# A decoder layer on one core: FFN up and gate token-major, 512 columns at a time, turned back by VectorE and small DMAs

## The chip, the cores and the metric

The kernel runs on one core of one Trainium2 chip. The metric is the device time of one execution in microseconds (us). Three executions of the kernel before took 447.74, 448.15 and 448.26 us, median 448.15. The trace comes from one more execution, with the profiler on, which took 447.88 us; the part of it that the instructions span is 446.0 us.

Engines are named as the profile names them: PE is TensorE's matmul stream, PEld its weight loads, DVE is VectorE, ACT is ScalarE, POOL is GpSimd, SP is SyncE. SPq is SP's queue, which issues nearly all DMAs.

## The reference

One layer of a decoder trunk, float32, 256 tokens (S), model width 1024 (D), FFN width 2816. The second half, which the change touches, is:

```python
    x = x + jnp.einsum('bsd,de->bse', merged, w_out[l])
    h = rmsnorm(x, norm2_g[l])
    up = causal_dwconv(jnp.einsum('bsd,df->bsf', h, w_up[l]), ffn_conv_w[l], ffn_conv_b[l])
    act = jax.nn.gelu(up) * jnp.einsum('bsd,df->bsf', h, w_gate[l])
    x = x + jnp.einsum('bsf,fd->bsd', act, w_down[l])
```

`causal_dwconv` is a convolution over three successive tokens, with its own three weights and bias per channel. The first half, called the mixers here, is a projection to 7168 columns, a gated linear recurrence (rx, rg, ri), an attention with 8 heads (q, k, v), two branch gates (ga, gb), two branch projections (pr, pa) and the output projection (wo).

## The kernel before, in words

**Precision.** Every float32 operand is split into a rounded part `hi` and the rest `lo`. Each product is three matmuls (`mm3`, lines 240 to 243): stationary hi with moving hi, hi with lo, lo with hi. A profile line L241, L242 or L243 is one of these three.

**The weight stream.** All weights come as 1 MB chunks, 128 partitions by 2048 columns, numbered in the order of use (`stream`, lines 173 to 198). For a chunk SP issues a load into a `raw` buffer (`load_next`, lines 203 to 213; 3 buffers), ScalarE casts it to `hi` (line 223; 4 buffers) and VectorE subtracts to get `lo` (line 224; 3 buffers). `advance(i)` (line 226) emits the loads and splits up to chunk `i`; loads are emitted up to 3 chunks ahead of the splits. A `raw` buffer becomes free when its chunk is split, a `hi` or `lo` buffer when TensorE has used the chunk.

**Two forms of matmul.** In the channel-major form (`fm_mm`, line 245) the weights are stationary (128x128) and the activations move, 256 tokens at a time: each matmul has 256 columns, and the result has channels on the partitions and tokens along the free axis. In the token-major form (`tm_mm`) the activations are stationary, 128 tokens at a time, and the weights move, 512 columns at a time; the result has tokens on the partitions. With `split=True` the 512 columns are two runs of 256 from one chunk, which holds half the contraction of two 256-column blocks (`two`, line 179). The mixers use the token-major form for q, k, v, ga, gb, pr and pa, the channel-major one for rx, rg and ri. The down projection and wo use `rows_mm` (line 664), 512 columns wide as well.

**The FFN** (lines 770 to 793). There are NF = 11 blocks of 256 channels. Block j does `up` (48 matmuls of 256 columns), `gate` (48), and then the down projection of block j-1 (24 matmuls of 512 columns), which adds into four PSUM banks `acc` that stay open to the end. `up_post` (line 740) multiplies `up` by the norm's factor per token (`rbf`, line 743), does the convolution along the free axis (one ScalarE pass, line 747, and two VectorE passes, line 751, per 128 channels) and the GELU (line 753). `gate_post` (line 756) multiplies by `gate` and splits the product into the operand of the down projection. All of this has channels on the partitions, where conv weights and biases are one number per partition. Block 0 is done in two halves of the contraction, since the last transposes of the normed activations (`norm2_t`, line 680) come between them; `norm2_bcast` (line 726) makes `rbf` with a small matmul.

**Order.** The mixers run as units of four quarters (`run_unit`). After each quarter, `run` emits the work that the table `AFTER` lists for it: `s24` is `advance(24)`, `P0` is an attention step, and so on. The table was written by an offline planner. Before the change it covers the mixers and wo; the FFN is a plain loop in which the splits run two chunks ahead (`AHEAD_S`). When the program is built, a list scheduler settles each engine's queue: emission order is the priority, and an instruction that is not ready by the builder's own reckoning lets later ones pass. Once built, each queue runs in its order.

**Buffers.** `half` is a pool of 22 buffers of 128x1024. PSUM has 4 banks in pool `psA` (long accumulations) and 4 in `psB` (`bank`).

Of the kernel before, what the change touches and what calls it, by code (L numbers as in the profile page):

```python
# [15 lines left out]
P = 128  # L16
S = 256
# [16 lines left out]
UNITS = ("rx0 rx1 rx2 rx3 rg0 rg1 rg2 rg3 k0 k1 k2 k3 ri0 q0 q1 ri1 q2 q3 v0 v1 v2 v3 ga0 ga1 ga2 ga3 gb0 "  # L34
         "gb1 gb2 gb3 pr0 pr1 pr2 pr3 pa0 pa1 pa2 pa3")
AFTER = {
    "rx0.0": "stats",
    "rg0.0": "s4",
    "rg0.2": "bcast evac1 s5",
    "rg0.3": "s6",  # L40
    "rg1.1": "evac0 evac2",
    "rg1.2": "evac3",
    "rg1.3": "conv0 decay",
    "rg2.0": "s7",
    "rg2.2": "conv1",
    "rg2.3": "s8 split0",
    "k0.1": "s9",
    "k0.2": "s10",
    "k0.3": "conv2 s11",
    "k1.0": "conv3 split1",  # L50
    "k1.3": "s12",
    "k2.3": "s13",
    "ri0.1": "s14",
    "ri0.2": "krs",
    "q0.0": "gelu1",
    "q0.1": "la0 lb0",
    "q0.2": "s15",
    "q1.0": "lc0",
    "q1.2": "s16",
    "q1.3": "s17",  # L60
    "ri1.0": "s18",
    "ri1.3": "ld0 la1",
    "q2.2": "lb1",
    "q3.1": "Tq0 ks0",
    "q3.2": "s19 ks1",
    "q3.3": "s20 qrs gelu0",
    "v0.2": "Tk0",
    "v0.3": "s21",
    "v2.0": "S0",
    "v2.1": "s22",  # L70
    "v2.2": "s23",
    "v3.1": "Tk1",
    "v3.3": "S1 S2",
    "ga0.2": "s24 P0",
    "ga0.3": "s25 lc1 s26 S3",
    "ga1.1": "P1 O0",
    "ga1.3": "Tq1",
    "ga2.1": "P2",
    "ga2.3": "P3",
    "ga3.0": "s27",  # L80
    "ga3.1": "O1",
    "ga3.2": "S6",
    "ga3.3": "S7 O3",
    "gb0.0": "O2 ya0 S4",
    "gb0.1": "S5",
    "gb0.2": "s28",
    "gb1.0": "P6",
    "gb1.2": "ld1 ya1 s29",
    "gb1.3": "P4",
    "gb2.0": "sa1",  # L90
    "gb2.1": "P7 O4",
    "gb2.2": "s30",
    "gb2.3": "ys1",
    "gb3.1": "ys0",
    "gb3.2": "P5",
    "gb3.3": "O6",
    "pr0.0": "s31 sb0",
    "pr0.1": "s32 O5",
    "pr0.2": "O7",
    "pr0.3": "s33",  # L100
    "pr1.2": "sa0",
    "pr2.2": "s34",
    "pr3.2": "s35",
    "pa0.0": "s36",
    "pa1.0": "s37",
    "pa1.3": "s38",
    "pa2.1": "s39",
    "pa2.3": "sb1",
    "pa3.2": "m0",
    "pa3.3": "m1 s40",  # L110
    "wo.3": "m3 s41",
    "wo.5": "m2",
    "wo.11": "n00",
    "wo.12": "s42 n10",
    "wo.15": "n01 s43",
}


# [1 line left out]
def trunk_layer(ctx: ExitStack, tc: tile.TileContext, xT, x, vec, win_fm, win_tm, wri, wpr, wpa,  # L120
# [10 lines left out]
    def half(name, dt=F32):  # L131
        return halfp.tile([P, 1024], dt, tag="half", name=name)
# [7 lines left out]
    def kt(t):  # L140
        return t.rearrange("p (k t) -> p k t", t=S)
# [49 lines left out]
    c_up, c_gt, c_dn = [], [], []  # L191
    for j in range(NF):
        c_up.append(add(wup[j]))
        c_gt.append(add(wgate[j]))
        if j >= 1:
            c_dn.append(add(wdown[j - 1]))
    c_dn.append(add(wdown[NF - 1]))
    last = len(stream) - 1

    raw, hi, lo = {}, {}, {}  # L200
# [56 lines left out]
    def fm_ps(name):  # L257
        return kt(bank(name))
# [421 lines left out]
    def norm2_t(t, hf):  # L680
        ps = bank(f"h2T{t}{hf}").rearrange("p (k t) -> p k t", k=4)
        ts = slice(t * P, (t + 1) * P)
        for k4 in range(4):
            k = 4 * hf + k4
            nc.tensor.transpose(ps[:, k4, :], xs[:, t, k * P:(k + 1) * P], ident)
        for k4 in range(4):
            k = 4 * hf + k4
            g = pv[:, V_G2 + k:V_G2 + k + 1]
            nc.scalar.activation(h2h[k][:, ts], ps[:, k4, :], AF.Copy, scale=g)
            nc.vector.scalar_tensor_tensor(h2l[k][:, ts], ps[:, k4, :], g, f(h2h[k][:, ts]),  # L690
                                           op0=OP.mult, op1=OP.subtract)
        nc.scalar.activation(small(f"sq2{t}{hf}", 512), xs[:, t, halves[hf]], AF.Square,
                             accum_out=ss2[:, hf, t:t + 1])
# [32 lines left out]
    def norm2_bcast():  # L726
        nc.vector.tensor_add(ss2[:, 0, :], ss2[:, 0, :], ss2[:, 1, :])
        rsqrt(ss2[:, 0, :], rs2, 1.0 / D, 2)
        for t in range(2):
            nc.vector.tensor_scalar(dg[:, t, :], ident, rs2[:, t:t + 1], None, op0=OP.mult)  # L730
        ps = bank("rbfp")
# [5 lines left out]
    acc = {(t, hf): psA.tile([P, 512], F32, tag="A", name=f"acc{t}{hf}") for t in range(2) for hf in range(2)}  # L737
    act = {}

    def up_post(j, ps):  # L740
        uc = half(f"fuc{j}")
        u, c = kt(uc[:, :512]), kt(uc[:, 512:])
        nc.vector.tensor_mul(u, ps, rbf2)  # L743
        for i in range(2):
            m = 2 * j + i
            w = lambda k: pv[:, V_FW + 3 * m + k:V_FW + 3 * m + k + 1]
            nc.scalar.activation(c[:, i, :], u[:, i, :], AF.Identity, scale=w(2),  # L747
                                 bias=pv[:, V_FB + m:V_FB + m + 1])
            for k in (1, 0):
                d = 2 - k  # L750
                nc.vector.scalar_tensor_tensor(c[:, i, d:], u[:, i, :S - d], w(k), c[:, i, d:],  # L751
                                               op0=OP.mult, op1=OP.add)
        nc.scalar.activation(c, c, AF.Gelu_apprx_tanh)
        return c

    def gate_post(j, c, ps):
        nc.vector.tensor_mul(c, c, ps)
# [12 lines left out]
    for j in range(NF):  # L770
        pu, pg = fm_ps(f"up{j}"), fm_ps(f"gt{j}")
        if j == 0:

            advance(c_up[0] + AHEAD_S)
            for half_k in range(2):
                ks = range(4 * half_k, 4 * half_k + 4)
                for ps, i in ((pu, c_up[0]), (pg, c_gt[0])):
                    fm_mm(ps, i, h2h, h2l, ks, True)
                    if not half_k and ps is pu:
                        norm2_t(1, 1)  # L780
            norm2_bcast()
            gate_post(0, up_post(0, pu), pg)
        else:
            advance(c_up[j] + AHEAD_S)
            fm_mm(pu, c_up[j], h2h, h2l)
            c = up_post(j, pu)
            advance(c_gt[j] + AHEAD_S)
            fm_mm(pg, c_gt[j], h2h, h2l)
            gate_post(j, c, pg)
            advance(c_dn[j - 1] + AHEAD_S)  # L790
            for t in range(2):
                for hf in range(2):
                    down(j - 1, t, hf)
    add_out(1, halves[1], acc[1, 1])
    advance(c_dn[NF - 1])
    for t in range(2):
# [75 lines left out]
```

## Time and profile before

| | us |
|---|---|
| median of 3 runs | 448.15 |
| profiled execution | 447.88 |
| its span | 446.0 |
| PE busy | 440.8 (99%) |
| DVE busy | 313.8 (70%) |
| ACT busy | 261.5 (59%) |
| mean DMA rate | 182 GB/s |

In a row of the timeline the columns are start, duration, engine, line, operation, output and inputs, tile sizes and count. In a row of the groups (lines) the columns are line, engine, operation, output and inputs, shapes, count, then busy us and mean ns of one, then the idle time of the engine just before these instructions and what ended it. Matmuls overlap each other in the array, so the distance between two starts, not the duration of one, is what a matmul costs.

### The profile page before, as it was taken

The numbers are of one execution on the slowest core, as the hardware profiler recorded it, in microseconds if no ns is written. First come the engines' busy times: TensorE is split into PE (matmuls) and PEld (weight loads), VectorE is DVE, ScalarE is ACT, GpSimd is POOL, SyncE is SP. The second block draws the span as 40 slices with busy tenths as digits, with TensorE's granted clock in tenths as the row PEclk, the third lists the DMA queues.
The fourth block names the chain that finished last, engine by engine and source line by source line (L and its number), as shares of the span: only waits on it lengthen the run. The fifth ranks groups of instructions, "written<-read, shape, count | busy, mean of one in ns | idle before, by whom it ended". The sixth has DMA issues, their size and how long they took to land.

```text
span 446.0 us, 6672 instructions
## 1 busy us (share of the span) xinstructions
PE 440.8 (99%) x2736; PEld 397.3 (89%) x2736; DVE 313.8 (70%) x462; ACT 261.5 (59%) x319; POOL 1.6 (0%) x9
## 2 busy tenths in 40 slices
PE   8999999999999999999999999999999999999996
PEld 8999988888888888888888899999999999999995
DVE  4688996979999775755677888575576575575553
ACT  4687757999996799733141656454354454454420
POOL 1000000000000000000000000000000000000000
PEclk9999999999999999999999999999999999999999
DMA  7995554645575455445545356545645645545202
GB/s 226 373 340 215 216 191 147 205 173 158 181 228 167 127 181 188 155 132 196 191 175 179 114 191 248 195 143 190 220 140 190 216 157 185 202 173 190 94 1 94
DMA packets 17629, 81.24 MB, mean 182 GB/s; under 512 B 1728, under 2 KB 4160, under 8 KB 10944
## 3 DMA queue, kind: packets, MB, share of 16 engines
q1 hardware_dynamic: 16880, 80.22, 51.9%
q10 hardware_dynamic: 720, 0.61, 0.5%
q8 instruction: 21, 0.34, 0.3%
q14 instruction: 8, 0.07, 0.0%
HBM read 79.78 MB, written 1.05 MB: 181 GB/s over the span
## 4 chain that ended last, share of the span: by engine, by line
PE 91%; ACT 5%; DMA 2%; issue 0%; DVE 0%; SPq 0%; ACTq 0%
PE gt L241 5%; PE gt L243 5%; PE gt L242 5%; PE up L243 5%; PE up L242 5%; PE up L241 5%; PE acc L241 4%; PE acc L242 4%; PE acc L243 4%; DMA raw<-in_win_fm 2%; PE rg L241 2%; PE rg L242 2%; PE rg L243 2%; PE ga L241 2%; PE gb L241 2%; PE pr L241 2%
## 5 line engine op out<-in xcount | busy, mean ns | idle before, releaser
L223 ACT CAST hi<-raw 128x2048 fp32r<-128x2048 f32 (+3 forms) x88 | 138.1, 1579 | 100.9 <-PE up L242 32.5
L224 DVE TENSOR_TENSOR lo<-raw,hi 128x2048 fp32r<-128x2048 f32 (+3 forms) x92 | 171.1, 1870 | 32.3 <-PE acc L242 14.0
L241 PE MATMUL up<-h2h,hi 128*128 128x256 f32 x176 | 49.9, 284 | 0.0
L241 PE MATMUL gt<-h2h,hi 128*128 128x256 f32 x176 | 49.9, 283 | 0.0
L243 PE MATMUL up<-h2h,lo 128*128 128x256 f32 x176 | 49.8, 283 | 0.0
L243 PE MATMUL gt<-h2h,lo 128*128 128x256 f32 x176 | 49.8, 283 | 0.0
L242 PE MATMUL gt<-h2l,hi 128*128 128x256 f32 x176 | 49.8, 283 | 0.0
L242 PE MATMUL up<-h2l,hi 128*128 128x256 f32 x176 | 49.8, 283 | 0.0
L241 PEld LDWEIGHTS up<-h2h,hi 128*128 128x128 f32 x176 | 33.7, 192 | 0.4
L242 PEld LDWEIGHTS up<-h2l,hi 128*128 128x128 f32 x176 | 33.7, 192 | 0.3
L242 PEld LDWEIGHTS gt<-h2l,hi 128*128 128x128 f32 x176 | 33.8, 192 | 0.0
L241 PEld LDWEIGHTS gt<-h2h,hi 128*128 128x128 f32 x176 | 33.8, 192 | 0.0
L243 PEld LDWEIGHTS gt<-h2h,lo 128*128 128x128 f32 x176 | 33.8, 192 | 0.0
L243 PEld LDWEIGHTS up<-h2h,lo 128*128 128x128 f32 x176 | 33.7, 192 | 0.0
L241 PE MATMUL acc<-hi,fa 128*128 128x512 f32 x86 | 33.6, 391 | 0.0
L242 PE MATMUL acc<-lo,fa 128*128 128x512 f32 x86 | 33.6, 390 | 0.0
L243 PE MATMUL acc<-hi,fa 128*128 128x512 f32 x86 | 33.5, 389 | 0.0
L743 DVE TENSOR_TENSOR fuc<-up,rbf 128x512 f32<-128x512 f32 x11 | 7.6, 691 | 33.2 <-PE up L243 33.2
L243 PEld LDWEIGHTS acc<-hi,fa 128*128 128x128 f32 x86 | 16.1, 188 | 3.5
L751 DVE SCALAR_TENSOR_TENSOR fuc<-fuc,pv 128x255 f32<-128x255 f32 (+1 forms) x44 | 18.6, 479 | 0.8 <-ACT fuc L747 0.7
L241 PEld LDWEIGHTS acc<-hi,fa 128*128 128x128 f32 x86 | 16.2, 188 | 3.1
L242 PEld LDWEIGHTS acc<-lo,fa 128*128 128x128 f32 x86 | 16.2, 188 | 2.9
(220 smaller groups left out, 1011.1 us busy)
## 6 DMA issues: line engine op xcount, KB each, us to landing
raw<-in_win_tm SPq DMA_DIRECT2D x12, 1024.0 KB, 4.8
raw<-in_win_fm SPq DMA_DIRECT2D x11, 1024.0 KB, 5.7
raw<-in_wup SPq DMA_DIRECT2D x11, 1024.0 KB, 4.8
raw<-in_wgate SPq DMA_DIRECT2D x11, 1024.0 KB, 4.8
raw<-in_wdown SPq DMA_DIRECT2D x11, 1024.0 KB, 4.8
raw<-in_wpr SPq DMA_DIRECT2D x4, 1024.0 KB, 4.9
raw<-in_wpa SPq DMA_DIRECT2D x4, 1024.0 KB, 4.9
raw<-in_wout SPq DMA_DIRECT2D x4, 1024.0 KB, 4.8
```

The lines of the kernel that those rows point to most:

```text
L223: (nc.vector.tensor_copy if on_dve else nc.scalar.copy)(hi[i][:, s], raw[i][:, s])
L224: nc.vector.tensor_sub(lo[i][:, s], raw[i][:, s], f(hi[i][:, s]))
L241: nc.tensor.matmul(o, ah, bh, start=start, stop=False, skip_group_check=skip)
L242: nc.tensor.matmul(o, ah, bl, start=False, stop=False, skip_group_check=skip)
L243: nc.tensor.matmul(o, al, bh, start=False, stop=stop, skip_group_check=skip)
L743: nc.vector.tensor_mul(u, ps, rbf2)
L751: nc.vector.scalar_tensor_tensor(c[:, i, d:], u[:, i, :S - d], w(k), c[:, i, d:], op0=OP.mult, op1=OP.add)
```

## The change

1. **Up and gate in pairs of blocks.** Ten of the eleven blocks are taken as five pairs of 512 channels. Each pair's `up` and `gate` use `tm_mm(..., split=True)`: per half of the contraction (`pair_half`) 24 matmuls of 512 columns. A chunk now holds half the contraction of two blocks (`two`). The last block stays channel-major (`last_block`).
2. **Turning back.** The result has tokens on the partitions, and the convolution wants channels there. `turn` has VectorE transpose each 32x32 block of the two PSUM banks into a buffer, and then 16 DMAs on SP move groups of 32 partitions by 256 elements (32 KB each) so that each channel's tokens land on that channel's partition. Ten turns make 20 VectorE transposes of 128x512 and 160 DMAs.
3. **The work behind.** `pair_up` multiplies by `rbf` in two passes of 128x512, does the convolution of four groups of 128 channels (`conv3`, the same instructions as before) and one GELU of 1024 columns. `pair_gate` multiplies by the turned gate in two passes and splits 1024 columns at once.
4. **Order.** The down projection of pair p-1 comes after `up` and `gate` of pair p, and that of the last pair after the last block. In pair 0 the order is up, gate, up, gate by halves of the contraction; otherwise both halves of up and then both of gate. The FFN now runs under the table too: `fu1` is `pair_up(1)`, `fg1` is `pair_gate(1)`, `n11` and `bcast2` are the last transposes and `norm2_bcast`, whose PSUM bank moves to `psA`. `acc` is allocated at the first down. The whole table, the mixers' part included, is written anew.

The diff, cut to its core (of the table some entries):

```diff
-    "rg0.0": "s4",
-    "rg0.2": "bcast evac1 s5",
+    "rg0.1": "bcast",
+    "rg0.2": "s5 evac1",
...
-    "q0.0": "gelu1",
-    "q0.1": "la0 lb0",
+    "k3.1": "s14 gelu1",
+    "q0.1": "la0 s16 lb0",
...
+    "up00.0": "n01",
+    "up00.1": "s44",
+    "up00.2": "n11",
+    "gt00.0": "bcast2",
...
+    "up11.1": "fu0 s49",
+    "up11.2": "fg0",
+    "gt10.0": "s50",
+    "gt11.1": "s51",
+    "gt11.3": "s52 fu1",
+    "dn0.2": "s53",
+    "up20.2": "fg1",
+    "up20.3": "s54",
+    "up21.1": "s55",
+    "gt20.0": "s56",
+    "gt21.0": "s57",
+    "gt21.3": "fu2 fg2",
+    "dn2.3": "s58",
+    "up30.0": "s59",
...
+    "gt31.2": "fu3 s63",
...
+    "dn5.2": "fg3",
...
+    "dn7.1": "s71 fu4",
+    "dn7.2": "fg4",
...
+    def turn(name, ps):
+        src, dst = half(f"{name}s"), half(f"{name}d")
+        v = src.rearrange("p (j t c b) -> p t c j b", j=4, t=2, c=4)
+        for t in range(2):
+            nc.vector.transpose(v[:, t], ps[t].rearrange("p (c j b) -> p c j b", c=4, j=4))
+        for i in range(4):
+            for j in range(4):
+                nc.sync.dma_start(dst[32 * j:32 * j + 32, i * 256:(i + 1) * 256],
+                                  src[32 * i:32 * i + 32, j * 256:(j + 1) * 256])
+        return dst.rearrange("p (i t c b) -> p t c i b", i=4, t=2, c=4)
...
+    def pair_up(p):
+        d = turned["up", p]
+        u, c = half(f"fu{p}"), half(f"fc{p}")
+        rb = rbf.rearrange("p (t i b) -> p t i b", t=2, i=4)
+        for t in range(2):
+            nc.vector.tensor_mul(tok32(u, t), d[:, t], rb[:, t, None].to_broadcast([P, 4, 4, 32]))
+        for i in range(4):
+            conv3(kt(c)[:, i, :], kt(u)[:, i, :], 4 * p + i)
+        nc.scalar.activation(c, c, AF.Gelu_apprx_tanh)
+        gated[p] = c
+
+    def pair_gate(p):
+        c, d = gated[p], turned["gt", p]
+        for t in range(2):
+            nc.vector.tensor_mul(tok32(c, t), d[:, t], tok32(c, t))
+        ah, al = half(f"fah{p}", F32R), half(f"fal{p}", F32R)
+        split2(ah, al, c)
...
+    def pair_half(kind, p, kh):
+        c = (c_up if kind == "up" else c_gt)[p, kh]
+        if not kh:
+            open_ps[kind, p] = [bank(f"{kind}{p}{t}") for t in range(2)]
+        advance(c)
+        for k4 in range(4):
+            tm_mm(open_ps[kind, p], c, 4 * kh + k4, k4, h2h, h2l, True)
+            if kh and k4 == 3:
+                turned[kind, p] = turn(f"f{kind}{p}", open_ps[kind, p])
+            yield
...
-    for j in range(NF):
-        pu, pg = fm_ps(f"up{j}"), fm_ps(f"gt{j}")
...
+    for p in range(NP):
+        for kind, kh in (("up", 0), ("gt", 0), ("up", 1), ("gt", 1)) if p == 0 else (
+                ("up", 0), ("up", 1), ("gt", 0), ("gt", 1)):
+            run(f"{kind}{p}{kh}", pair_half(kind, p, kh))
+        if p:
+            run(f"dn{2 * p - 2}", downs(2 * p - 2))
+            run(f"dn{2 * p - 1}", downs(2 * p - 1))
+    run("last", last_block())
+    run(f"dn{NF - 3}", downs(NF - 3))
+    run(f"dn{NF - 2}", downs(NF - 2))
```

More of the change, by code (lines that the diff above doesn't have):

```diff
@@ new lines @@
+    "rg3.1": "s8",
+    "k0.0": "s9",
+    "k0.1": "conv2",
+    "k0.2": "conv3",
+    "k0.3": "split1",
+    "k1.0": "s10",
+    "k1.3": "s11",
+    "k2.1": "s12",
+    "k2.2": "s13",
+    "k3.1": "s14 gelu1",
+    "ri0.2": "krs",
+    "ri0.3": "s15",
+    "q0.1": "la0 s16 lb0",
+    "q1.1": "s17",
+    "q1.3": "lc0",
+    "ri1.0": "s18",
+    "q2.0": "ld0",
+    "q2.1": "s19",
+    "q2.2": "la1",
+    "q3.0": "lb1 Tq0",
+    "q3.1": "ks0",
+    "q3.2": "gelu0",
+    "v0.1": "qrs",
+    "v0.3": "s20 Tk0",
@@ new lines @@
+    "pr2.0": "sa1 O6",
+    "pr2.2": "O5",
+    "pr3.3": "sb1",
+    "pa0.0": "s35 s36",
+    "pa0.3": "s37",
+    "pa1.0": "s38",
+    "pa2.1": "s39",
+    "pa2.2": "s40 m0",
+    "pa3.3": "m1",
+    "wo.3": "s41",
+    "wo.4": "m2",
+    "wo.6": "m3",
+    "wo.11": "n10 s42",
+    "wo.12": "n00",
+    "wo.14": "s43",
+    "up00.0": "n01",
+    "up00.1": "s44",
+    "up00.2": "n11",
+    "gt00.0": "bcast2",
+    "gt00.2": "s45",
+    "up01.2": "s46",
+    "up01.3": "s47",
+    "gt01.3": "s48",
@@ L116 @@
+    "up41.3": "s68",
+    "dn6.0": "s69",
+    "dn6.1": "s70",
+    "dn7.1": "s71 fu4",
+    "dn7.2": "fg4",
+    "last.2": "s72",
+    "dn9.0": "s73",
+    "dn9.3": "s74",
 }
@@ L734, in norm2_bcast, with ffn_mm, conv3 @@
         nc.scalar.copy(rbf, ps[:, :S])
-    acc = {(t, hf): psA.tile([P, 512], F32, tag="A", name=f"acc{t}{hf}") for t in range(2) for hf in range(2)}
-    act = {}
+    acc, act = {}, {}
+    def ffn_mm(ps, i, kh):
+        for k4 in range(4):
+            tm_mm(ps, i, 4 * kh + k4, k4, h2h, h2l, True)
+    def turn(name, ps):
[8 more added lines that the diff above has]
+        return dst.rearrange("p (i t c b) -> p t c i b", i=4, t=2, c=4)
+    tok32 = lambda a, t: a.rearrange("p (c t i b) -> p t c i b", t=2, i=4, b=32)[:, t]
+    def conv3(c, u, m):
+        w = lambda k: pv[:, V_FW + 3 * m + k:V_FW + 3 * m + k + 1]
+        nc.scalar.activation(c, u, AF.Identity, scale=w(2), bias=pv[:, V_FB + m:V_FB + m + 1])
+        for k in (1, 0):
+            d = 2 - k
+            nc.vector.scalar_tensor_tensor(c[:, d:], u[:, :S - d], w(k), c[:, d:], op0=OP.mult, op1=OP.add)
+    turned, gated = {}, {}
+    def pair_up(p):
[14 more added lines that the diff above has]
+        split2(ah, al, c)
+        for i in range(2):
+            act[2 * p + i] = tuple(kt(a[:, i * 512:(i + 1) * 512]) for a in (ah, al))
     def up_post(j, ps):
@@ L768, in add_out @@
         nc.vector.scalar_tensor_tensor(xs[:, t, cs], ps, rs2[:, t:t + 1], xs[:, t, cs], op0=OP.mult, op1=OP.add)
-    for j in range(NF):
-        pu, pg = fm_ps(f"up{j}"), fm_ps(f"gt{j}")
[L772 to L793, printed above, removed]
+    for p in range(NP):
+        item[f"fu{p}"] = lambda p=p: pair_up(p)
+        item[f"fg{p}"] = lambda p=p: pair_gate(p)
@@ new lines, in downs, with last_block @@
+    def downs(j):
+        advance(c_dn[j])
+        for t in range(2):
+            for hf in range(2):
+                if j == 0:
+                    acc[t, hf] = psA.tile([P, 512], F32, tag="A", name=f"acc{t}{hf}")
+                down(j, t, hf)
+                yield
+    def last_block():
+        pu, pg = fm_ps("upl"), fm_ps("gtl")
+        for ps, i in ((pu, c_up[NP]), (pg, c_gt[NP])):
+            advance(i)
+            for j in range(2):
+                for h in range(2):
+                    fm_mm(ps, i, h2h, h2l, range(4 * h, 4 * h + 4), js=(j,))
+                    if j and h:
+                        if ps is pu:
+                            c = up_post(NF - 1, pu)
+                        else:
+                            gate_post(NF - 1, c, pg)
+                    yield
```

132 lines of the change are left out of this document (53 added, 79 removed).

## The prediction

> **What bounds the kernel now.** I read the page first: engine totals, granted clock, and the engines' shares of the chain that ended last.
>
> ```profile
> span 446.0 us, 6672 instructions
> PE 440.8 (99%) x2736; PEld 397.3 (89%) x2736; DVE 313.8 (70%) x462; ACT 261.5 (59%) x319; POOL 1.6 (0%) x9
> PEclk9999999999999999999999999999999999999999
> PE 91%; ACT 5%; DMA 2%; issue 0%; DVE 0%; SPq 0%; ACTq 0%
> ```
>
> TensorE has work for 440.8 of 446.0 us, at full clock, and 91% of the last chain is its own matmuls. The next view cuts the span into windows: the mixers in two parts, the start of the FFN, and one steady FFN block. After the window's length come PE, PEld, DVE, ACT and POOL with their busy time, then clock, DMA share and GB/s.
>
> ```profile
> core 0: us, PE busy (x) PEld busy (x) DVE busy (x) ACT busy (x) POOL busy (x), PEclk, DMA share, GB/s
> 12.50:100.00 87.50, 87.45 (x569) 80.31 (x569) 73.79 (x129) 68.98 (x84) 0.00 (x0) 1.00 0.63 231
> 100.00:254.50 154.50, 154.39 (x767) 129.41 (x766) 115.28 (x177) 99.45 (x137) 0.00 (x0) 1.00 0.52 171
> 254.50:284.00 29.50, 29.50 (x228) 28.54 (x227) 24.51 (x46) 19.19 (x26) 0.00 (x0) 1.00 0.55 192
> 284.00:301.00 17.00, 17.00 (x122) 16.04 (x121) 10.28 (x11) 7.87 (x7) 0.00 (x0) 1.00 0.52 182
> ```
>
> From 12.5 us on TensorE never waits for more than crumbs (0.05 and 0.11 us in the mixers, 0.00 in the FFN). So the time can fall only if the matmuls themselves take less, and it rises by whatever wait the new arrangement lets through. In the steady block VectorE has 10.28 of 17.0 us, ScalarE 7.87, and what they wait for there is TensorE, the cushion of the FFN. From the waits (us in total, times, longest):
>
> ```profile
> DVE fuc L743 <- PE up L243: 33.2, 9, 3.7
> ACT hi L223 <- PE up L242: 32.5, 9, 3.7
> ```
>
>
> Busy time does not show what a matmul costs, since successive ones overlap (each lists 0.28 or 0.39 us). The distance between starts does. The TensorE timeline, first matmul of each run:
>
> ```profile
> 207.81 0.39 PE L241 MATMUL pa<-hi,ybh 128*128 128x512 f32 x1
> ...
> 228.21 0.60 PE L590 MATMUL mT<-ident,sgb 128*128 128x128 f32 x4
> ...
> 278.50 0.40 PE L241 MATMUL acc<-hi,fa 128*128 128x512 f32 x1
> ...
> 283.96 0.28 PE L241 MATMUL up<-h2h,hi 128*128 128x256 f32 x1
> ...
> 289.72 0.28 PE L241 MATMUL gt<-h2h,hi 128*128 128x256 f32 x1
> ```
>
> Forty-eight `up` matmuls of 256 columns take 289.72 - 283.96 = 5.76 us, 0.1200 each. Twenty-four `acc` matmuls of 512 take 5.46 us, 0.2275 each. The 90 `pa` matmuls from 207.81 to 228.21 take 0.2267 each, and they have the very form that `up` and `gate` get: activations stationary, weights moving as two runs of 256 columns from one raw layout (the split form of `tm_mm`).
>
> **The change, part by part.**
>
> *Matmuls.* Ten of the eleven blocks go from 10 x 2 x 48 = 960 matmuls of 256 columns to 480 of 512. Before: 960 x 0.1200 = 115.2 us. After: 480 x 0.2267 to 0.2275 = 108.8 to 109.2 us. The gain is 6.0 to 6.4 us; I take 6.1. All of it lies on the path, since TensorE never waits here. Block 11, the down matmuls and the ending keep their forms.
>
> The Trainium skill (TensorE: Matmul & The Clock Gate, section Back-to-back issue gap) states a gap of N/2.4 + 2.5 ns at full clock, so that two halves would cost only 2.5 ns more than one whole matmul. An estimate from that page is 480 x 2.5 ns = 1.2 us of gain, and a profiled 447.4 us in place of my 442.5. The rows here do not agree: 2 x 120.0 - 226.7 = 13.3 ns, five times as much, so the measurement decides.
>
> *VectorE.* The groups by line and shape (busy us, mean ns of one):
>
> ```profile
> L224 DVE TENSOR_TENSOR lo<-raw,hi 128x2048 fp32r<-128x2048 f32 x68 | 155.5, 2286 | 28.2 <-PE acc L242 14.0 <-issue 4.9 <-PE k L242 2.3
> L751 DVE SCALAR_TENSOR_TENSOR fuc<-fuc,pv 128x255 f32<-128x255 f32 x22 | 9.8, 479 | 0.7 <-ACT fuc L747 0.7
> L757 DVE TENSOR_TENSOR fuc<-fuc,gt 128x512 f32<-128x512 f32 x11 | 7.6, 686 | 12.3 <-PE gt L243 12.3
> L224 DVE TENSOR_TENSOR lo<-raw,hi 128x1024 fp32r<-128x1024 f32 x4 | 4.9, 1222 | 1.3 <-ACT hi L223 1.3
> L223 ACT CAST hi<-raw 128x1024 fp32r<-128x1024 f32 x4 | 4.2, 1050 | 0.0
> ```
>
> A pair of blocks now asks of VectorE: six weight subtractions, 6 x 2.29 = 13.7; four turns of 128x512 out of PSUM; four multiplications of 128x512, 4 x 0.69 = 2.7; eight conv steps, 8 x 0.48 = 3.8; one split of 1024 columns, 1.2. No row shows a turn by 32x32 blocks. It reads and writes as many elements as L757, so I take 0.69 each; the ends are 0.48 (the shortest row here) and 2.29 (four times the elements). That makes 21.4 + 2.8 = 24.2 us in a pair that lasts 6 x 24 x 0.2273 = 32.7 us (74%); with the upper end 30.6 (93%), still under TensorE. So the turns cost nothing while TensorE covers them; without the cover, 20 x 0.69 = 13.8 us. The Trainium skill (VectorE: DVE Perf Modes, section The three transpose paths) gives 311 ns for 128x128 bf16; an estimate of four of those is 1.24 us a turn and 26.4 us a pair, still covered. ScalarE does the same work in longer instructions.
>
> *The small DMAs.* Each turn issues 16 DMAs of 32 KB on SP, 160 in all, in the queue that also issues the weights. Nearest rows, SP's timeline and the issues with KB each and us to landing:
>
> ```profile
> 0.74 0.37 SPq L283 DMA_DIRECT2D xT<-in_xT  x1
> 1.16 0.90 SPq L286 DMA_DIRECT2D raw<-in_win_fm  x2
> 2.10 0.43 SPq L283 DMA_DIRECT2D xT<-in_xT  x1
> ...
> 13.47 3.14 SPq L286 DMA_DIRECT2D raw<-in_win_fm  x4
> 16.94 13.06 SPq L213 DMA_DIRECT2D raw<-in_win_fm  x5
> ```
>
> ```profile
> raw<-in_wup SPq DMA_DIRECT2D x11, 1024.0 KB, 4.8
> raw<-in_wpr SPq DMA_DIRECT2D x4, 1024.0 KB, 4.9
> out<-xs SPq DMA_DIRECT2D x8, 128.0 KB, 1.9
> xT<-in_xT SPq DMA_DIRECT2D x3, 256.0 KB, 5.5
> ```
>
> At best SP issues one per (2.10 - 0.74)/3 = 0.45 us; in the crowded opening 23 DMAs took from 0.74 to 16.94, 0.70 each. A turn is thus 1.4 us of VectorE, 16 x 0.45 = 7.3 us of issue and 1.9 us to the last landing, 10.6 us; at the crowded end 1.4 + 11.2 + 5.5 = 18.1. I take 11, because the queue carries only six loads a pair beside them. When is it wanted? Matmuls run in units of 5.46 us (24 of them). `fu1` and `fu2` stand two units (10.9 us) after their turn, `fu3`, `fg0`, `fg3` and `fg4` 9.6, `fu0` 13.6, `fg1` 15, `fu4` 19, and the down that needs a pair comes four to six units after its gate turn. An 11 us turn leaves VectorE waits of a us or two. Queued behind such a wait stand the weight subtractions; TensorE feels them only when one is later than the two units of lookahead that three `lo` buffers give. A weight load behind a burst of 16 is late by 7.3 us and lands in 4.8, 12.1 in all, with its split three units (16.4 us) off: hidden. The loads' new two-run layout moves from 4.8 to 4.9: nothing. Traffic: 32 x 32 KB, one MB more per pair beside six, so the DMA share of 0.52 rises to about 0.61: nothing.
>
> *Where a stall can come.* In pair 2 `fg2` stands directly behind its own turn, and the split for the next `up` (`s58`) after it. If VectorE's queue keeps that order, the turn lands 10.6 us after `gt21` ends, two multiplications (1.4) and the subtraction (2.3) follow, and `up30`, due at 10.9, starts 3.4 us late. If `s58` goes ahead, 0. I take 0.3, since the builder orders by readiness. At the FFN's start `gt00` needs the two PSUM banks of the last transposes, issued 4.1 us into `up00` and drained by four of ScalarE's evictions, 1.5 us, with VectorE beside them: needed at 5.5, so 0 to 1, taken as 0.2.
>
> ```profile
> L689 ACT ACTIVATE h2h<-h2T,pv 128x128 fp32r<-128x128 f32 x16 | 5.5, 365 | 2.3 <-DVE h2l L690 1.8 <-PE h2T L685 0.6
> ```
>
> *The mixers' rewritten order.* TensorE idles 0.16 us there, so it can gain nothing. Its tightest place, in the chain that ended last:
>
> ```profile
> 96.13 1.28 ACT L402
> ...
> 97.90 1.80 ACT hi L223
> 99.70 0.37 ACT rt L402
> ...
> 100.49 0.66 PE Tq L485 x4
> ```
>
> ScalarE, with table loads of 1.28, leads there and TensorE just meets it. One more table load, or one late split (1.80 + 2.29), would cost 1.3 to 4.1; none costs 0. I take 0.2, nearest to the 0.16 row, because TensorE's dense rows lie all around it.
>
> **Sum**, against the profiled execution (447.88 us, span 446.0): 447.88 - 6.1 + 0.3 + 0.2 + 0.2 = 442.5. The median of the runs, 448.15, stands 0.27 above that execution, so I name 442.8. Bounds: all gain and no stall 441.5; all stalls at their ends (3.4 + 1 + 4.1) 450.3.
>
> **The rivals.**
>
> (1) *One stall, not many*: `fg2`'s order or the ScalarE-led stretch lets 1.5 to 4 us through. 444 to 446.5. For it: only two units of lookahead, 83% VectorE at the FFN's start. Against: the rows show the cushions unspent.
>
> (2) *Slower: the turns' landing paces VectorE.* Place: SP's queue. With 0.70 us per DMA both turns of a pair lie back to back: from the end of `up`, 1.4 + 2 x 11.2 + 5.5 = 29.3 us, that is 18.4 after `gate` ends (10.9 later). `fg` then holds VectorE from 15 to 18.4; two multiplications (1.4), ScalarE's cast (1.05), the split (1.22) and the weight subtraction (2.29) end at 24.4, but the chunk so split is due four units after `gate`, at 21.8. That is 2.6 us in pair 1; taken for all four boundaries, 10.4: 442.5 + 10.4 = 452.9. It decides from a landing about 17.4 us after `gate` ends (1.5 us a pair eats the 6.1). For it: the opening's rows. Against: there the rings were full of loads; in the FFN their share is 0.52.
>
> (3) *The wide form gains little.* A wide run broken by transposes is slower:
>
> ```profile
> 146.34 0.48 PE L241 MATMUL ga<-hi,xgh 128*128 128x512 f32 x1
> ...
> 149.18 0.49 PE L530 MATMUL pt<-ident,sm 128*128 128x128 f32 x3
> ```
>
> Twelve matmuls in 2.84 us are 0.2367 each; at that rate 480 cost 113.6, a gain of 1.6: 447.0 with the stalls above; at 0.2400 none, 447.9. Against: the unbroken `pa` run. The 1.2 us that the Trainium skill's page on TensorE gives above falls in this case, as its smaller part (0.02), since the trace contradicts it.
>
> **How the numbers follow.** My forecast (441.5 to 444) 0.53; rival 1 0.14; rival 3 0.06, half of it within 0.2% of 448.15 (0.9 us, about what a measurement can tell from no change); rival 2 0.27, since its price rests on the least known row, of which 0.01 ends within 0.2%. Faster 0.53 + 0.14 + 0.03 = 0.70, same 0.04, slower 0.26. The range starts at 441.3, just below the best sum. Up to 449 it holds 0.74; the mild end of rival 2, up to 451, brings it to 0.8. My own case alone is 441.5 to 444.
>
> **What would show it.** Right: 48 `up` matmuls of 512 columns in about 10.9 us; TensorE without gaps; VectorE near 74% in a pair; turn DMAs spaced about 0.45 us; span near 440.6. Wrong: gaps before `up` or `gt` released by L224 or ScalarE's cast, VectorE waiting for the turned tile longer than about 6 us, turns far above 0.69 us, or a stall between 75 and 110 us.

## The result: 461.04 us, slower by 2.9%

The changed kernel takes 461.04 us (median of four runs, 460.19 to 461.56) beside 448.20 us (median of four) for the kernel before. The ratio is 1.0285, 95% interval 1.0265 to 1.0306. The forecast was 442.8 us, with a range of 441.3 to 451.0: both the sign and the range missed.

The profiled execution took 461.56 us. From its page: the span, the engine totals, PE's busy tenths and the granted clock in 40 slices, and the engines' shares of the chain that ended last.

```profile
span 459.8 us, 5937 instructions
PE 441.1 (96%) x2256; PEld 374.1 (81%) x2256; DVE 326.6 (71%) x477; ACT 261.0 (57%) x309; POOL 1.5 (0%) x9
PE   8999999999999999999999999999589999969986
PEclk9999999999999999999999999999979999989999
PE 40%; DMA 24%; SPq 13%; DVE 10%; ACT 9%; issue 2%; ACTq 0%; DVEq 0%
```

Before, 91% of that chain was TensorE's own matmuls; now it is 40%, and a queue that was at 0% has 13%. The lost time is not spread out: PE has two dents, and the clock falls in the same places. The windows put a length on them (us of the window, then PE, PEld, DVE, ACT, POOL busy, clock, DMA share, GB/s; first the start of the FFN, then about two pairs):

```profile
255.39:284.00 28.61, 28.61 (x133) 23.77 (x132) 20.10 (x36) 14.27 (x17) 0.00 (x0) 1.00 0.51 162
284.00:317.00 33.00, 32.78 (x145) 26.79 (x144) 22.46 (x25) 13.91 (x13) 0.00 (x0) 1.00 0.52 179
317.00:350.00 33.00, 26.76 (x106) 20.91 (x105) 20.90 (x22) 12.83 (x10) 0.00 (x0) 0.90 0.56 184
```

TensorE's timeline shows what a run of 48 wide matmuls costs, and what the worst one lost. These are the first matmul of `up` 2, of its gate, the resumption after the gap, two in the slow stretch, and the first `down` behind it:

```profile
311.76 0.39 PE L285 MATMUL up<-hi,h2h 128*128 128x512 f32 x1
...
322.64 0.61 PE L285 MATMUL gt<-hi,h2h 128*128 128x512 f32 x2
...
333.67 1.22 PE L285 MATMUL gt<-hi,h2h 128*128 128x512 f32 x2 [4.28 <-ACT hi L267]
336.00 0.80 PE L286 MATMUL gt<-lo,h2h 128*128 128x512 f32 x1 [1.10 <-DVE lo L268]
...
337.44 0.63 PE L287 MATMUL gt<-hi,h2l 128*128 128x512 f32 x1
337.87 0.63 PE L285 MATMUL gt<-hi,h2h 128*128 128x512 f32 x1
...
342.92 0.39 PE L285 MATMUL acc<-hi,fah 128*128 128x512 f32 x1
```

Undisturbed, 48 matmuls take 322.64 - 311.76 = 10.88 us, as forecast, and every run of them that does not wait takes just that. The gate of pair 2 takes 342.92 - 322.64 = 20.28, or 9.4 too many. The trace sums the same way over the FFN: gate 2 +9.4, gate 4 +5.8, gate 3 +1.1, the last downs +1.5, the last block's gate +0.6, the first downs +0.5, together 18.9 us. The FFN starts 0.9 us later than before (255.39 against 254.53; these are two single traces, and the runs below that keep the new order of the mixers start it anywhere from 254.06 to 255.49). So 446.0 - 6.1 + 0.9 + 18.9 = 459.7, the span. The gain is there in full, and three times as much is lost to a few waits.

What do they wait for? From the waits (us in total, times, longest):

```profile
ACT hi L267 <- DMA raw<-in_wup: 20.4, 7, 9.0
ACT hi L267 <- DMA raw<-in_wgate: 15.7, 7, 4.1
...
PE gt L285 <- ACT hi L267: 6.5, 2, 4.3
...
PE gt L286 <- DVE lo L268: 4.4, 4, 1.6
DVE fc L825 <- DMA fgt3d<-fgt3s: 4.0, 1, 4.0
...
DVE fu L816 <- DMA fup1d<-fup1s: 3.1, 1, 3.1
...
DVE fc L825 <- DMA fgt0d<-fgt0s: 2.9, 1, 2.9
```

Read from the bottom: VectorE waits for turned tiles; TensorE waits for a cast, and the cast for a weight load. Before, no weight cast in the FFN waited for anything but TensorE. Beside the row for `up` that the prediction shows, the waits of the kernel before had only these two:

```profile
ACT hi L223 <- PE acc L243: 26.8, 9, 3.2
...
ACT hi L223 <- PE gt L242: 5.5, 10, 1.0
```

SP's queue around the big dent shows why the load was late (start, time from the first to the end of the last, count):

```profile
302.62 10.79 SPq L796 DMA_DIRECT2D fup1d<-fup1s  x16
313.51 0.53 SPq L252 DMA_DIRECT2D raw<-in_wgate  x1
314.14 11.20 SPq L796 DMA_DIRECT2D fgt1d<-fgt1s  x16
325.44 0.53 SPq L252 DMA_DIRECT2D raw<-in_wgate  x1
```

The chain that ended last runs through exactly these: burst, load, burst, load, cast, subtraction.

```profile
313.42 0.05 issue
313.51 6.22 DMA raw<-in_wgate
319.75 0.51 SPq L796
...
325.44 6.20 DMA raw<-in_wgate
331.72 1.91 ACT hi L267
333.65 2.30 DVE lo L268
```

The second load goes out directly behind sixteen small DMAs, lands 6.2 us later, is cast in 1.9, and TensorE, which wanted it at 329.2, resumes at 333.67.

The chain also shows that a burst is not all price. One DMA of the second burst goes out at 319.75 because the first load has just landed. In this trace no DMA of SP's queue goes out before the one eight places ahead of it has landed, in all 255 cases. In eight of the ten bursts a small DMA waits so for a weight load (us in total, times, longest), and a burst takes 10.0 to 12.4 us:

```profile
SPq L796 <- DMA raw<-in_wgate: 4.7, 4, 2.4
```

### The profile page after: what moved, and what is told of

It reads as the page before. It is cut to its first block, busy times and chain, and to the rows that moved or that the text cites. A ratio compares the mean times of both kernels' runs of the same rounds, so it can differ in the third digit from the quotient of the medians.

```text
span 459.8 us, 5937 instructions
## 1 busy us (share of the span) xinstructions
PE 441.1 (96%) x2256; PEld 374.1 (81%) x2256; DVE 326.6 (71%) x477; ACT 261.0 (57%) x309; POOL 1.5 (0%) x9
## 2 busy tenths in 40 slices
DMA packets 27868, 86.46 MB, mean 188 GB/s; under 512 B 4288, under 2 KB 11840, under 8 KB 23744
## 4 chain that ended last, share of the span: by engine, by line
PE 40%; DMA 24%; SPq 13%; DVE 10%; ACT 9%; issue 2%; ACTq 0%; DVEq 0%
SPq L796 13%; DMA raw<-in_wgate 10%; DMA raw<-in_win_fm 5%; DVE lo L268 5%; ACT hi L267 4%; DMA raw<-in_wup 4%; DMA raw<-in_wdown 2%; DVE xa L429 2%; PE gb L285 2%; PE pr L285 2%; PE ga L285 2%; PE yo L287 2%; PE gb L287 2%; PE pr L286 2%; PE yo L285 2%
## 5 line engine op out<-in xcount | busy, mean ns | idle before, releaser
L268 DVE TENSOR_TENSOR lo<-raw,hi 128x2048 fp32r<-128x2048 f32 (+3 forms) x92 | 171.0, 1869 | 43.7 <-ACT hi L267 25.8
L285 PE MATMUL gt<-hi,h2h 128*128 128x512 f32 x80 | 32.0, 409 | 6.5 <-ACT hi L267 6.5
L286 PE MATMUL gt<-lo,h2h 128*128 128x512 f32 x80 | 33.3, 417 | 4.4 <-DVE lo L268 4.4
L287 PE MATMUL gt<-hi,h2l 128*128 128x512 f32 x80 | 32.4, 407 | 0.0
L286 PE MATMUL acc<-lo,fah 128*128 128x512 f32 x80 | 31.3, 391 | 1.1 <-DVE lo L268 1.1
L287 PE MATMUL acc<-hi,fal 128*128 128x512 f32 x80 | 31.3, 391 | 0.2 <-DVE fal L282 0.2
L285 PE MATMUL up<-hi,h2h 128*128 128x512 f32 x80 | 31.3, 391 | 0.0
L286 PE MATMUL up<-lo,h2h 128*128 128x512 f32 x80 | 31.2, 390 | 0.0
L285 PE MATMUL acc<-hi,fah 128*128 128x512 f32 x80 | 30.8, 391 | 0.4 <-ACT hi L267 0.4
L287 PE MATMUL up<-hi,h2l 128*128 128x512 f32 x80 | 31.2, 389 | 0.0
L285 PE MATMUL rx<-xgh,hi 128*128 128x256 f32 x64 | 18.5, 289 | 0.5 <-ACT hi L267 0.5
L286 PE MATMUL rg<-xgl,hi 128*128 128x256 f32 x64 | 18.1, 283 | 0.0
L287 PE MATMUL rg<-xgh,lo 128*128 128x256 f32 x64 | 18.1, 283 | 0.0
```

The source lines that it names most:

```text
L268: nc.vector.tensor_sub(lo[i][:, s], raw[i][:, s], f(hi[i][:, s]))
L285: nc.tensor.matmul(o, ah, bh, start=start, stop=False, skip_group_check=skip)
L286: nc.tensor.matmul(o, ah, bl, start=False, stop=False, skip_group_check=skip)
L287: nc.tensor.matmul(o, al, bh, start=False, stop=stop, skip_group_check=skip)
```

## The experiments

One cause and two paths had to be told apart. The cause: the sixteen DMAs of a turn keep SP's queue for some 10 us. The paths: **late loads** (a weight load stands behind a burst, and its split comes late) and a **held VectorE** (a turned tile lands late; the multiplication that wants it holds VectorE's queue, with splits and the next transposes behind it). The rivals were the two paths one by one, the traffic itself, and the rest of the change (transposes, order table).

### No small DMAs

```diff
-        src, dst = half(f"{name}s"), half(f"{name}d")
+        src = dst = half(f"{name}s")
...
-        for i in range(4):
-            for j in range(4):
-                nc.sync.dma_start(dst[...], src[...])
```

> The turns' 160 DMAs are left out: the multiplications read the 32x32-transposed tile as it is, so channels stand on the wrong partitions and the FFN's output is not the reference's; all matmuls, VectorE and ScalarE work stays. Both theories: the stalls in the FFN vanish, and what is left is the wide matmuls' gain and the mixers' new order, 448.0 - 6.1 + 0.9 = 442.8 us. A third theory (C: the new order of splits and the later down projection are themselves late, whatever the DMAs do): above 448 us.

Measured: 442.27 us, ratio 0.987 (0.9849 to 0.989), span 440.9. Every run of 48 takes 10.88 us. So all that the change loses lies in the small DMAs, in their issue or in their landing, since the edit removes both. Transposes, multiplications, order and wide matmuls together keep a gain of 448.13 - 442.27 = 5.9 us, where the forecast had 6.1. The windows of the same two pairs as above:

```profile
284.00:317.00 33.00, 33.00 (x148) 27.32 (x147) 28.09 (x34) 19.59 (x19) 0.00 (x0) 1.00 0.58 196
317.00:350.00 33.00, 33.00 (x147) 27.36 (x146) 23.50 (x25) 15.76 (x13) 0.00 (x0) 1.00 0.58 198
```

TensorE is busy without a gap, and VectorE for 28.09 + 23.50 of 66.0 us, 78%.

### The small DMAs from GpSimd's queue

```diff
-                nc.sync.dma_start(dst[...], src[...])
+                nc.gpsimd.dma_start(dst[...], src[...])
```

> The 160 small DMAs of the turns are issued by GpSimd instead of SP; nothing else changes. Theory A (SP's queue: a turn's 16 DMAs occupy SP for 10.2 us at 0.635 each, and weight loads that stand behind them come late, so the split and then the matmul come late): the loads issue at once, the 9.4, 5.8 and 1.1 us stalls before the gate chunks shrink below 3 in all, time 443 to 447 us if GpSimd needs no longer per DMA than SP. Theory B (a turn lands late and holds VectorE, whose queue is in order, so splits and later turns come late; the loads are late only because the splits are): the latency of a turn is about the same, so most of the 19 us of stalls stays, 455 to 461 us, and VectorE's waits for the turned tiles stay near 3 us each.

Measured: 457.26 us, ratio 1.0211 (1.017 to 1.0251). The loads are free of the bursts, yet little comes back: turns land 15.6 to 29.5 us after their matmuls, and VectorE waits longer for them than in the changed kernel, where the longest wait was 4.0.

```profile
DVE fu L816 <- DMA fup4d<-fup4s: 8.8, 1, 8.8
DVE fu L816 <- DMA fgt2d<-fgt2s: 8.3, 1, 8.3
```

### The weight loads from GpSimd's queue

```diff
+FIRST = 46
-            nc.sync.dma_start(raw[i]..., stream[i])
+            (nc.gpsimd if i >= FIRST else nc.sync).dma_start(raw[i]..., stream[i])
```

> The weight loads of the FFN from the fifth chunk on are issued by GpSimd instead of SP; the turns' DMAs stay on SP at their pace. Theory A: no load stands behind a turn any more, and the turns wait for no load's turn in the queue: stalls below 4 us in all, 443 to 448 us. Theory B: the turns' latency (16 x 0.635 + 1.9, some 12 us) is what it was, VectorE still waits for each, time 454 to 461 us.

Measured: 461.32 us, ratio 1.0287 (1.0249 to 1.0324). No load stands behind a burst now. Gate 2 is back at 10.88 us, but `up` 4 takes 18.29 and the last block's gate 11.07 in place of 5.76. The waits show the other path:

```profile
DVE fu L817 <- DMA fup3d<-fup3s: 9.0, 1, 9.0
DVE fu L817 <- DMA fgt2d<-fgt2s: 9.0, 1, 9.0
```

At the largest stall VectorE stands 8.99 us for `fup3d`, until 381.81; the subtraction that TensorE wants starts behind that work at 387.13, and TensorE, idle for 4.75 us, resumes at 389.47. Casts still wait for loads here (5.3 us at most), and GpSimd issues many of those loads only when a subtraction has freed their buffer. So a load that stands behind a burst is not the whole explanation: with none left, the same time is lost through VectorE.

### The turned tiles wanted later

The multiplications stand some three units later in the table, held behind the last weight subtraction; the sixteen DMAs stay on SP.

```diff
-    "up11.1": "fu0 s49",
-    "up11.2": "fg0",
+    "up11.1": "s49",
+    "up11.2": "fu0",
...
+        with tc.issue_after(subs[-1]):
             for t in range(2):
                 nc.vector.tensor_mul(tok32(u, t), d[:, t], ...)
```

> The turns' 160 DMAs stay on SP as they are. Only the use is moved: the first multiplications of each pair (by the norm's factor, and by the gate) are emitted some three units of 24 matmuls after their turn's matmuls have ended, and held behind the last weight subtraction emitted before them, so that VectorE meets them when the turn has landed. Theory B (the landing holds VectorE's in-order queue, and everything behind it, the next turns' transposes too, comes late): VectorE's waits on the turned tiles (some 3 us each, 24 in all) go to nearly nothing, transposes start within 2 us of their matmuls' end instead of up to 12, time 443 to 449 us. Theory A (bursts on SP hold the weight loads): the bursts are as long, so the loads come late as before, 455 to 462 us.

Measured: 475.33 us, ratio 1.0614 (1.0599 to 1.0628), outside both expected ranges. VectorE's waits for turned tiles shrink to four of 0.7 to 3.8 us, and it is the worst kernel of all:

```profile
DVE lo L269 <- ACT hi L268: 52.0, 14, 10.2
...
ACT hi L268 <- DMA raw<-in_wgate: 31.4, 8, 9.7
```

Now the loads come late, since the bursts are still ahead of them: the gates of pairs 3 and 4 take 17.1 and 18.1 us, and behind the gate of pair 1 TensorE stands 6.0 us for a cast. A part of the loss is this edit's own: the downs wait 8.5 us for a product that now comes later.

### Both at once

The two edits above together: loads from GpSimd, tiles wanted later.

> Both halves are freed at once: FFN weight loads issued by GpSimd, so that no load stands behind a burst on SP, and the turned tiles' first multiplications later, behind the weight split, so that VectorE isn't held by a landing. Each half alone gave no gain (461.3 with the loads moved, 475.3 with the use later). Theory (the 10.2 us burst costs through late loads AND through a held VectorE, each able to keep the loss alone): the stalls ahead of the gate's chunks go, what is left is the down matmuls that come before their activations are ready: 444 to 452 us. Rival (it is the small DMAs' traffic itself that delays the loads, whichever queue issues them): casts still wait for loads, above 457 us.

Measured: 447.37 us, ratio 0.9995 (0.9965 to 1.0025), with runs from 445.02 to 451.13; why they spread so is open. Two edits that alone gave 461.3 and 475.3 give back 13.7 us together. Of the FFN's stalls some 3.5 us are left in the trace, at the first downs (a product that comes late) and the last ones; the trace is of the fastest run, 445.02. Both paths are real, each can keep the loss alone, and the traffic itself is not the cause: the same 160 DMAs run beside the same loads.

### The same bytes in eight DMAs

```diff
-        for i in range(4):
+        for i in range(2):
             for j in range(4):
-                nc.sync.dma_start(dst[32 * j:32 * j + 32, i * 256:(i + 1) * 256], ...)
+                nc.sync.dma_start(dst[32 * j:32 * j + 32, i * 512:(i + 1) * 512], ...)
```

> Each turn moves the same 512 KB in 8 DMAs of 64 KB in place of 16 of 32 KB. With two blocks per DMA the data land in wrong places, so the output is not the reference's. If SP's 0.635 us is a price per DMA and not per byte, a turn's burst falls from 10.2 to 5.1 us and its landing from about 12 to 7 us after it could start; theories A and B both expect most of the 19 us of stalls gone, 443 to 449 us. If bytes or rows set the price, the burst stays near 10 us and the time near 461.

Measured: 442.61 us, ratio 0.989 (0.9861 to 0.992), no stalls. SP's queue in the same place as above:

```profile
298.88 5.31 SPq L797 DMA_DIRECT2D fup1d<-fup1s  x8
304.29 0.53 SPq L252 DMA_DIRECT2D raw<-in_wgate  x1
304.92 6.31 SPq L797 DMA_DIRECT2D fgt1d<-fgt1s  x8
```

A DMA of 64 KB costs SP 5.31/8 = 0.66 us, one of 32 KB 10.79/16 = 0.67; from start to start the median within the bursts is 0.633 in both runs. SP pays by the DMA, not by the byte.

### The same bytes in twelve DMAs

```diff
+            n = 2 if i % 2 else 4
-            for j in range(4):
+            for j in range(n):
+                w, k = 1024 // n, (i + j) % 4
...
+                nc.sync.dma_start(dst[32 * i:32 * i + 32, j * w:(j + 1) * w], ...)
```

> The 512 KB of a turn in twelve DMAs, eight of 32 partitions x 256 columns and four of 32 x 512, all on SP; the blocks land in wrong places, so the output isn't the reference's, and only the time is read. Theory: a burst of 12 x 0.635 = 7.6 us, between eight DMAs (5.1 us, 442.6 us in all) and sixteen (10.2 us, 461 us). If the loss grows in proportion above the 5.1 us it is half of 18.4 us: 452 us; if it has a threshold near ten us of burst, 443 to 446 us. Rival (many small descriptors, not their count on SP): near 455 us, since the bytes in 256-column pieces fall by half only.

Measured: 442.33 us, ratio 0.9881 (0.9854 to 0.9908), one stall of 0.6 us. This is the sharpest comparison here, since VectorE's and ScalarE's instructions stand in the same order as in the changed kernel: four DMAs fewer in each burst are worth 18.7 us. SP's queue and the longest waits for a turned tile:

```profile
298.25 8.24 SPq L798 DMA_DIRECT2D fup1d<-fup1s  x12
306.58 0.53 SPq L252 DMA_DIRECT2D raw<-in_wgate  x1
...
316.80 0.53 SPq L252 DMA_DIRECT2D raw<-in_wgate  x1
```

```profile
DVE fc L827 <- DMA fgt3d<-fgt3s: 2.0, 1, 2.0
DVE fu L818 <- DMA fup1d<-fup1s: 0.9, 1, 0.9
```

Two bursts and two loads take 316.80 + 0.53 - 298.25 = 19.1 us; with sixteen they take 325.44 + 0.53 - 302.62 = 23.4. They also begin 13.2 us after the last matmul of `up` 1 in place of 9.7, because VectorE is already behind. The loss is not proportional to the burst (that would have been 452 us): it has an edge between twelve and sixteen. That beyond it the lateness of one turn is passed to the next is what the landings below suggest; no run isolates it.

### The burst dealt to two queues

```diff
-                nc.sync.dma_start(dst[...], src[...])
+                (nc.sync if (i + j) % 2 else nc.gpsimd).dma_start(dst[...], src[...])
```

> The sixteen DMAs of a turn are dealt in turn to SP's queue and GpSimd's, eight each; the work is the same. Theory (the length of the burst on a queue decides): 8 x 0.635 = 5.1 us on SP beside as much on GpSimd, turns land before VectorE needs them and loads come in time, 443 to 449 us, the upper part if GpSimd's DMAs land as late as they did when it issued all sixteen (16 to 29 us after the matmuls). Rival (sixteen small DMAs cost what they cost, wherever they are issued): 455 to 461 us.

Measured: 441.77 us, ratio 0.986 (0.9846 to 0.9875), no stalls. It has the lowest median of all the runs, though not clear of 442.27 and 442.33, and is 1.4% faster than the kernel before. SP's queue, then GpSimd's:

```profile
298.60 5.77 SPq L796 DMA_DIRECT2D fup1d<-fup1s  x8
304.46 4.97 SPq L796 DMA_DIRECT2D fgt1d<-fgt1s  x8
```

```profile
327.27 3.91 POOL L796 DMA_DIRECT2D fup2d<-fup2s  x8 [19.78 <-DVE fup2s L793]
```

The number of small DMAs is the changed kernel's; only the length of the burst on any one queue is halved. The order of VectorE's queue differs in places here, so the clean proof is the run before this one, but the two agree. The turns land 9 to 18 us after their matmuls, as they do with eight DMAs on one queue (8 to 16).

### The turn through device memory

```diff
+        through = scratch.tile([P, 1024], F32, tag="turn", name=f"{name}x")
+        nc.sync.dma_start(through, src)
+        rows = through.rearrange("(i b) (j n) -> j b i n", i=4, j=4)
+        for j in range(4):
+            nc.sync.dma_start(dst[32 * j:32 * j + 32].rearrange("b (i n) -> b i n", i=4), rows[j])
```

> A turn goes through device memory: one DMA of 512 KB out and four of 128 KB back (32 partitions each) in place of 16, all on SP. SP's occupancy falls from 10.2 to about 5 x 0.6 = 3 us a turn; the latency is some 2 for the way out, 4 x 0.6 and 2 to 3 for the way back, 7 us instead of 12. Theories A and B both expect most of the stalls gone, 443 to 448 us; under B the gain is less where one turn's way back waits for its way out at the head of SP's queue while loads stand behind it (up to 3 us a turn).

Measured: 444.96 us, ratio 0.9932 (0.9917 to 0.9947). Five DMAs in place of sixteen; a turn's two legs land after each other, yet nothing on VectorE waits for them. Stalls of 3.6 us in all are left.

> The turn through device memory (one DMA out, four back), issued by GpSimd instead of SP, so that no weight load stands behind a way back that waits for its way out. The run with these on SP gave 445.0 us with 1.8 us of stall after the second gate, 0.8 at the last block and 0.7 in the last downs. If SP's waits cause these, 442.5 to 444 us; if GpSimd's issue is slower than SP's and the landing later, 445 to 448.

The same five DMAs from GpSimd's queue: 449.82 us, above both expected ranges, ratio 1.0024 (1.0 to 1.0049), with runs from 445.95 to 457.51. Nothing is gained by freeing SP of five DMAs, and I have no explanation for the spread.

### The order table

> The kernel before with the new table for the mixers and wo only; the FFN is the old one. The changed kernel's FFN starts 0.9 us later than that of the kernel before, which makes 449.0 us if the table is the cause; if it is the noise of loads in the crowded opening, 448.0 to 448.3.

The kernel before with only the mixers' part of the table replaced: 448.6 us beside 447.86, ratio 1.0016 (1.0007 to 1.0024), or 0.7 us, between the two expected values. Its trace starts the FFN at 254.59, only 0.06 us after the kernel before, so the 0.7 us rests on the medians and its place is not shown.

> The turn through device memory (one DMA out, four back, on SP) with the mixers' and wo's part of the order table as it was before the change; the FFN's part is the new one. Theory: the turn through memory gave 444.96 us, and the new table of the mixers costs 0.7 us by its own run, so 444.2 us (443.6 to 444.8), ratio 0.991. Rival (the new table of the mixers belongs to the new FFN's start, and the old one delays it): 445 us or more.

The reverse, the turn through memory with the mixers' old table, was to win those 0.7 us and missed: 455.6 us, ratio 1.0172 (1.0151 to 1.0194). TensorE's timeline has one gap:

```profile
308.49 0.80 PE L284 MATMUL acc<-hi,fah 128*128 128x512 f32 x1 [9.38 <-ACT fah L280]
```

The builder settles the queues anew for every table, and here it put one more weight subtraction ahead of the first pair's multiplications. They start at 295.74 in place of 290.57, and the first `down` waits for their product. A table's part cannot be priced by itself: 0.7 us in one kernel, 10.6 us the other way in the other.

## Why the prediction was wrong, point by point

**The step that failed** is *The small DMAs*, in its price and in its rule of cover. It took 0.45 us for each, a burst of 7.3, a turn of 11, "VectorE waits of a us or two", and a load behind a burst "12.1 in all, with its split three units (16.4 us) off: hidden".

- *Price.* Measured 0.633 us from start to start (median), 0.63 to 0.77 with the waits for landings, a burst of 10.0 to 12.4. The 0.70 of the crowded opening, kept as the upper end, was the better row. The run with twelve DMAs shows how much hung on it: its burst of 8.2 us is close to the 7.3 forecast, and its 442.33 us to the 442.8.
- *Cover of the loads.* Burst 11.2 (1.3 of it the wait for the load before it to land), landing 6.2 in place of 4.8 (three held loads go out within 1.5 us of each other, and the DMA share is 1.00 from 329.0 to 333.1): 17.4 us against a cover of 16.4, and 1.9 more for the cast, which the step left out. With the forecast's own terms it was hidden by 4 us, with the measured ones it is late.
- *One turn at a time.* The step priced a turn by itself. The first one landed 13.0 us after its matmuls, 2.4 above the 10.6 worked out; the others after 18.4 to 26.3, since bursts queue behind each other and behind loads, and a VectorE that waits 3 us turns the next tile later (`up` 1 is transposed 11.8 us after its last matmul). Nothing in the sum let lateness carry over.

**Rival 2**, "the turns' landing paces VectorE", named the right place, SP's queue, and the right DMA price (0.70), and was given 0.27. Its edge was a landing 17.4 us after the gate's last matmul. The five gate turns landed at 18.7, 26.3, 19.2, 22.4 and 18.4, all beyond it; with twelve DMAs at 14.5, 18.6, 17.9, 17.3 and 12.7, about it or below. Its size was wrong: 10.4 us in four equal parts, where 18.9 came in unequal ones. It saw only the held VectorE, not the late loads, and the runs show that both had to be removed.

**The matmuls** were right: 10.88 us for 48, forecast 10.9. The rule of the Trainium skill weighed there (TensorE: Matmul & The Clock Gate, section Back-to-back issue gap) would have left 1.2 of the 6.1 us; the run without small DMAs, 5.9 us under its own before, bears out the rows instead. The Trainium skill gives that formula for an isolated gap and says that a stream of weight loads and matmuls departs from it, which the prediction left out. **Rival 3** falls with it.

**VectorE's turns** were right. The timeline, from the changed kernel:

```profile
301.29 1.31 DVE L793 STREAM_TRANSPOSE fup1s<-up 128x512 f32<-128x512 f32 x2
```

That is 0.66 us each, taken as 0.69. VectorE's share in two pairs without stalls is 78% (the run without small DMAs), forecast 74%; it never became the bound by its work.

**The small stalls**: `fg2` behind its own turn, the PSUM banks at the FFN's start and rival 1's single stall were looked for in the wrong places; none of them shows when the bursts are short. **The mixers' table** was taken at 0.2 and measures 0.7 us by its own run.

**What would show it wrong** was listed rightly: gaps before `gt` released by the cast and by L268's subtraction are what the waits show. VectorE's wait stayed under the 6 us named there (4.0); the loss came at a smaller wait than that.

**Added to it, not foreseen**: the clock. After the gap of 4.28 us the matmuls stand 337.87 - 337.44 = 0.43 us apart, twice the usual 0.2267, until 340.0, and the window's granted clock is 0.90. The 24 matmuls from 333.67 on take 9.25 us in place of 5.44; the gap of 1.10 accounts for 1.3 of that, so some 2.5 of gate 2's 9.4 us are matmuls at the slow clock. The Trainium skill (TensorE: Matmul & The Clock Gate, section What's actually happening) says that an idle stretch of about 3.4 us halves the clock and that as long a busy one restores it. The trace agrees for this gap: the granted clock is 0.50 from 333.06, 3.7 us after TensorE fell idle, to 339.89, 3.9 us after the gap of 1.10. In gate 4 two shorter ones close together did the same:

```profile
406.23 0.73 PE L285 MATMUL gt<-hi,h2h 128*128 128x512 f32 x2 [2.19 <-ACT hi L267]
408.55 0.80 PE L286 MATMUL gt<-lo,h2h 128*128 128x512 f32 x1 [1.59 <-DVE lo L268]
```

Single gaps of 1.69 us (ahead of the first downs in the run with both edits) and of 2.22 us (in `up` 4 with the small DMAs on GpSimd) did not.

## What to carry to other kernels

Count the DMAs that a step puts on a queue, price each by the queue's own crowded rows, and lay the whole burst in front of every load that shares the queue: the issuing time can be the bound while the bytes are not. A wait that is hidden when priced alone can pass its edge when the same queue serves the next one late, so price two successive turns, not one, and look for the edge. When a burst hurts, make it shorter (fewer, larger DMAs, or two queues) before moving it: moved whole to GpSimd's queue, it still made the turns land late (457.26 us).

## What the runs showed of the hardware

- A DMA from on-chip memory to on-chip memory over 32 partitions takes SP 0.633 us from start to start (median within the bursts), alike for 32 and 64 KB; with the waits for landings it comes to 0.62 (4.97/8) to 0.79 (6.31/8). Weight loads in the FFN of the kernel before, each alone in the queue, stand at 0.33, and the four reads of a turn through memory took 1.76 in a row, 0.44 each:

```profile
306.83 1.76 SPq L799 DMA_DIRECT2D fup1d<-fup1x  x4
```

- Those reads also write 32 partitions each, so it isn't the target alone that makes 0.63; what does stays open. From GpSimd the same DMAs took 0.49 (3.91/8; 0.487 in the median, in both runs that issue them there).
- On SP's queue no DMA of the changed kernel went out before the one eight places ahead of it had landed (255 cases of 255), while some did go out before the one seven places ahead had. So a slow load holds the queue once more when eight DMAs are in flight.
- The Trainium skill (DMA: Bandwidth & Descriptors, section Anatomy of one DMA, told there for transfers that GpSimd issues) puts the fixed cost at about 2.0 us, most of it the receipt after the data has moved, with some 50 ns for the sequencer's dispatch. The landing agrees in the median, 1.9 to 2.2 us from issue in all ten turns, though single DMAs behind a load took up to 7.0. That the issuing engine is held for ten times that dispatch and more (0.49 us on GpSimd, 0.63 on SP) is what decided this case.
- The turns through device memory moved 5.2 MB more in all (91.68 against 86.46 MB) and were still faster than sixteen direct DMAs on one queue, 444.96 against 461.04 us.
